# A transformer layer on one core: joining two products of one weight part into one 512-column matmul, and making two weight sums by accumulating DMA

## The chip, the cores and the metric

The kernel runs on one core of a Trainium2 chip. The metric is the device time of one execution in microseconds (us). Of the kernel before there are three runs, and beside them one profiled execution with its trace.

## The reference

One layer of a decoder on 512 tokens with 2048 features, in float32. What matters here is that nearly all of it is products of weights with activations:

```python
h    = rmsnorm(x, attn_norm_g)
proj = h @ w_in                      # 2048 -> 9216: u, v_sgu, q, k, v_att, g_a, g_b
y_a  = chunked_spatial_gating(gelu(u), rmsnorm(gelu(v_sgu)), w_s, b_s)
y_b  = stick_breaking_attention(rmsnorm(q), rmsnorm(k), v_att)
x    = x + (sigmoid(g_a) * (y_a @ w_up_a) + sigmoid(g_b) * (y_b @ w_up_b)) @ w_o
h    = rmsnorm(x, ffn_norm_g)
x    = x + (silu(h @ w_gate_half) * (h @ w_up_half)) @ w_ffn_out     # 2048 -> 2 * 5632 -> 2048
ple  = p @ w_ple
x    = x + sigmoid(rmsnorm(x, ple_norm_g) @ w_ple_gate) * ple
```

## The kernel before

Activations lie with features in partitions and tokens along the row. Every float32 operand is split into two float32r parts, high and low (`hi`, `lo`; `whi`, `wlo` for weights), and every product is three matmuls that add up in PSUM (`mm3`, L244 to L247): high weights by high activations, high weights by low activations, low weights by high activations. The first two have the same stationary operand.

A *unit* is two row tiles (256 rows) of the contraction, an output *pair* is two tiles of 128 features by 512 tokens. A plain unit (kind P) is four block products of 512 columns, so 12 matmuls. A Strassen unit (kind S) is seven half-size products of 256 columns in Winograd's form, so 21 matmuls. For it the weights become seven blocks of 128 columns: three as they are loaded, four that are sums. There are 766 Strassen units: 264 in the combined projection, 32 in the output projection, 344 in the first feed-forward product, 91 in the three passes of the second, 35 in the last gate. The other products are plain.

Weights come two units at a time (a *double*). `Weights` (L273) issues one DMA of 512 KB (L255) on the sync engine's queue (SP) into one of three raw blocks, and then, in steps that are interleaved with those of the next double: ScalarE (ACT) copies the three loaded blocks to `whi` (L312, 128x768), VectorE (DVE) makes two sums (L292, 128x512), subtracts for `wlo` (128x768), makes the third sum (128x256) and the fourth (L321, 128x256), ACT copies the four sums to `whi` (L323, 128x1024), and DVE makes their `wlo` (128x1024). A slot is a raw block with its `whi` and `wlo`; there are three, and the next DMA into a raw block waits until DVE has read it. `next_weights` (L345) prepares up to two doubles ahead.

`Pair.add` (L525) issues the matmuls. A Strassen pair keeps products P1 and P6 in PSUM bank `psp`, P7 and P4 in `psq`, P2 and P3 in `psy`, P5 in half of `psr`; `psy`, `psp`, `psq` exist twice, `psr` and `small` once, which makes eight banks. When the Strassen units of a pair are all issued, `mix` (L549) joins the products to the outputs: two copies by ACT (L553, L554) and four operations of DVE (L555 to L560), then `rest` adds the bank `psy` (L584).

Work beside the products (attention, gating, norms, forms of the activations) is issued by `tick`, once a unit, and kept behind that unit on each engine. A scheduler orders the instructions of each engine by their place in the program and by priorities; `Weights.to` raises the priority of the weights' steps.

Of the kernel before, what the change touches and what calls it, by code (L numbers as in the profile page):

```python
# [12 lines left out]
F32 = mybir.dt.float32  # L13
# [17 lines left out]
# Units by Strassen's products (S) and by plain ones (P) where they are mixed.  # L31
# [5 lines left out]
WHOLES = 13056  # L37
# [12 lines left out]
#   C11 = P1 + P2   C12 = P1 - P6 + P5 + P3   C21 = P1 - P6 + P7 - P4   C22 = P1 - P6 + P7 + P5  # L50
# A unit of the weights lies in DRAM as [A21 | A22 | A11 | A12].
# [3 lines left out]
def hybrid_layer(  # L55
# [5 lines left out]
    w_in: bass.AP,  # L61
    wsT: bass.AP,
# [16 lines left out]
    psm = ctx.enter_context(tc.tile_pool(name="psm", bufs=2, space=PSUM))  # L79
# [6 lines left out]
    # ---- SBUF that the phases share out among themselves: operands of float32r products in one  # L86
    # ---- tile, everything else in another
# [11 lines left out]
    class Arena:  # L99
# [4 lines left out]
        def take(self, n, how="low"):  # L104
            """Up from the bottom, at the lowest of the equal places, or down from the top."""
# [32 lines left out]
    def fits(sizes):  # L138
        """Whether these blocks can be had, with some room left over."""
# [17 lines left out]
    banks = iter(range(1 << 30))  # L157
    count = iter(range(1 << 30))
    psr = psa.tile([P, T], F32, name="psr")
    r_banks = [psr]  # L160

    def bank():
        tag = ("psy", "psp", "psq")[next(banks) % 3]
        return psm.tile([P, T], F32, tag=tag, name=nm(tag))
# [17 lines left out]
    def tick():  # L182
        """One unit more is issued. What is due now stays behind it on every engine."""
# [16 lines left out]
    class Staged:  # L200
        """The steps of a generator, one a unit, or all at once when the result is asked for."""
# [47 lines left out]
    slots = deque()  # L249

    def weight_tiles(src):
        """A slot, to be put back once its products are issued, with the weights as they are."""
        slot = slots.popleft()
        raw = slot[0].f(0, src.shape[1])
        nc.sync.dma_start(out=raw, in_=src)  # L255
        return slot, raw, slot[1], slot[2]
# [16 lines left out]
    class Weights:  # L273
# [10 lines left out]
        def steps(self):  # L284
# [9 lines left out]
            def nothing():  # L294
                pass
# [990 lines left out]
```

## Time and profile before

| | |
|---|---|
| Runs | 2731.14, 2731.86, 2733.67 us; median 2731.86 |
| Profiled execution, its span from the first to the last instruction | 2735.7 us |
| TensorE (PE) busy / weight loads (PEld) | 2714.8 / 2566.8 us, 19616 each |
| VectorE (DVE), ScalarE (ACT), GpSimd (POOL) busy | 2173.4, 1273.9, 68.4 us |
| DMA moved | 378.56 MB, read from DRAM 328.23 MB |

Three rates say what to look for in the trace: how far apart matmuls start (their busy times overlap, so the busy share of PE says little), how far apart DVE's instructions start, and how long a DMA takes from its issue until it has landed. The stages follow one another: the combined projection with attention under it up to about 790 us, the merging of the branches and the output projection to about 1230 us, the first feed-forward product to about 2090 us, the three passes of the second to about 2590 us, then the gate.

### The profile page before, as it was taken

Reading aid. Unit: us, or ns where it says so; the run is one execution under the profiler, and the core shown is the slowest. Engines: PE = TensorE matmul, PEld = TensorE weight load, DVE = VectorE, ACT = ScalarE, POOL = GpSimd, SP = SyncE. Lnnn points to the kernel's source line nnn. Section 1 sums busy time; section 2 is a strip of 40 time slices with the busy share of each in tenths; the row PEclk is TensorE's granted clock in tenths of the full one; section 3 lists DMA queues with packets and bytes.
Section 4 is the critical chain, followed back from the end, with each engine's and each line's share of the span. In section 5 each row is a group of like instructions: output and inputs, shape, how many; then the busy total and the mean of one; then the engine's idle time right before and its main releaser. Section 6 shows DMA issues by size and latency. Waiting matters only on the chain.

```text
span 2735.7 us, 48535 instructions
## 1 busy us (share of the span) xinstructions
PE 2714.8 (99%) x19616; PEld 2566.8 (94%) x19616; DVE 2173.4 (79%) x3457; ACT 1273.9 (47%) x1950; POOL 68.4 (2%) x130
## 2 busy tenths in 40 slices
PE   9999999999999999999999999999999999999999
PEld 7899999999998889989999999999999998988898
DVE  7677778787887667698888888888889677788887
ACT  7645555554544333374443444444345344343533
POOL 0100001010100000000000000000000000000000
PEclk9999999999999999999999999999999999999999
DMA  5333333333335444454333333333334445465654
GB/s 197 103 122 101 111 99 108 108 109 116 108 111 186 144 145 155 144 196 142 114 121 116 119 119 117 118 118 119 118 119 158 158 140 174 161 216 193 219 170 143
DMA packets 114416, 378.56 MB, mean 138 GB/s; under 512 B 12816, under 2 KB 15120, under 8 KB 114192
## 3 DMA queue, kind: packets, MB, share of 16 engines
q1 hardware_dynamic: 114192, 375.47, 42.8%
q8 instruction: 153, 2.51, 0.4%
q14 instruction: 71, 0.58, 0.1%
HBM read 328.23 MB, written 47.19 MB: 137 GB/s over the span
## 4 chain that ended last, share of the span: by engine, by line
issue 50%; PE 46%; DVE 1%; DMA 1%; ACT 1%; POOL 0%; POOLq 0%; DVEq 0%; ACTq 0%; SPq 0%
PE psy L245 5%; PE psy L246 5%; PE psy L247 5%; PE psq L247 4%; PE psp L247 4%; PE psq L246 4%; PE psp L246 4%; PE psp L245 4%; PE psq L245 4%; PE psr L247 1%; PE psr L245 1%; PE psr L246 1%; PE small L246 1%; PE small L247 1%; PE small L245 1%
## 5 line engine op out<-in xcount | busy, mean ns | idle before, releaser
L292 DVE TENSOR_TENSOR wlo<-wholes,whi 128x1024 fp32r<-128x1024 f32 (+3 forms) x943 | 991.2, 1054 | 365.7 <-ACT whi L312 291.0
L312 ACT ACTIVATE whi<-wholes 128x768 fp32r<-128x768 f32 (+1 forms) x397 | 327.1, 824 | 687.5 <-issue 333.6
L245 PE MATMUL psy<-parts,whi 128*128 128x256 f32 (+1 forms) x1956 | 600.4, 307 | 7.1 <-ACT whi L301 6.1
L246 PE MATMUL psy<-parts,whi 128*128 128x256 f32 (+1 forms) x1956 | 600.2, 307 | 0.0
L247 PE MATMUL psy<-parts,wlo 128*128 128x256 f32 (+1 forms) x1956 | 599.2, 306 | 0.0
L245 PE MATMUL psp<-parts,whi 128*128 128x256 f32 (+1 forms) x1706 | 516.4, 303 | 0.5 <-ACT whi L323 0.5
L247 PE MATMUL psp<-parts,wlo 128*128 128x256 f32 (+1 forms) x1706 | 502.0, 294 | 1.8 <-DVE wlo L292 1.8
L247 PE MATMUL psq<-parts,wlo 128*128 128x256 f32 (+1 forms) x1702 | 500.3, 294 | 2.0 <-DVE wlo L292 2.0
L246 PE MATMUL psp<-parts,whi 128*128 128x256 f32 (+1 forms) x1706 | 501.0, 294 | 0.0
L246 PE MATMUL psq<-parts,whi 128*128 128x256 f32 (+1 forms) x1702 | 500.7, 294 | 0.2 <-DVE parts L242 0.2
L245 PE MATMUL psq<-parts,whi 128*128 128x256 f32 (+1 forms) x1702 | 500.5, 294 | 0.0
L292 DVE TENSOR_TENSOR wholes<-wholes 128x256 f32<-128x256 f32 (+2 forms) x794 | 427.2, 538 | 5.5 <-DMA wholes<-w_gate 2.5
L323 ACT ACTIVATE whi<-wholes 128x1024 fp32r<-128x1024 f32 (+1 forms) x397 | 403.7, 1017 | 14.0 <-DVE wholes L321 14.0
L245 PEld LDWEIGHTS psy<-parts,whi 128*128 128x128 f32 x1956 | 374.3, 191 | 22.8 <-ACT whi L301 6.1
L247 PEld LDWEIGHTS psy<-parts,wlo 128*128 128x128 f32 x1956 | 374.2, 191 | 16.9
L246 PEld LDWEIGHTS psy<-parts,whi 128*128 128x128 f32 x1956 | 374.3, 191 | 15.9 <-DVE parts L242 0.7
L245 PEld LDWEIGHTS psp<-parts,whi 128*128 128x128 f32 x1706 | 326.5, 191 | 12.8 <-issue 1.7
L246 PEld LDWEIGHTS psp<-parts,whi 128*128 128x128 f32 x1706 | 326.3, 191 | 12.3 <-issue 1.7
L247 PEld LDWEIGHTS psp<-parts,wlo 128*128 128x128 f32 x1706 | 325.9, 191 | 9.6 <-DVE wlo L292 2.4
L247 PEld LDWEIGHTS psq<-parts,wlo 128*128 128x128 f32 x1702 | 326.0, 192 | 9.3 <-DVE wlo L292 2.8
L246 PEld LDWEIGHTS psq<-parts,whi 128*128 128x128 f32 x1702 | 325.9, 192 | 8.0 <-DVE parts L242 1.2
L245 PEld LDWEIGHTS psq<-parts,whi 128*128 128x128 f32 x1702 | 325.9, 191 | 7.2 <-issue 0.2
(139 smaller groups left out, 3369.8 us busy)
## 6 DMA issues: line engine op xcount, KB each, us to landing
wholes<-w_ffn_in SPq DMA_DIRECT2D x176, 512.0 KB, 3.9
wholes<-w_in SPq DMA_DIRECT2D x132, 512.0 KB, 3.9
wholes<-w_ffn_out SPq DMA_DIRECT2D x73, 512.0 KB, 3.7
wholes<-w_o SPq DMA_DIRECT2D x32, 512.0 KB, 4.1
wholes<-x SPq DMA_DIRECT2D x32, 512.0 KB, 5.3
wholes<-w_gate SPq DMA_DIRECT2D x25, 512.0 KB, 5.0
hid<-out SPq DMA_DIRECT2D x44, 256.0 KB, 2.0
wholes<-hid SPq DMA_DIRECT2D x22, 512.0 KB, 4.3
```

Source lines behind the costliest of these rows:

```text
L245: nc.tensor.matmul(ps, sh, mh, start=start, stop=False)
L246: nc.tensor.matmul(ps, sh, ml, start=False, stop=False)
L247: return nc.tensor.matmul(ps, sl, mh, start=False, stop=stop)
L292: return nc.vector.tensor_tensor(out=out, in0=a, in1=b, op=ALU.subtract)
L312: in_turn(nc.scalar.activation(h[:, :, 0:3], raw[:, :, 1:4], AF.Copy))
L323: nc.scalar.activation(h[:, :, 3:7], s, AF.Copy))
```

## The change

**Products.** In five of the seven Strassen products (P1, P6, P7, P5, P4) the matmuls of the high weights with the high and with the low activations become one of 512 columns, whose moving operand is a two-piece pattern over both parts (`both`). Each such product has a PSUM bank of its own: the left half takes high by high and low by high, the right half high by low. P2 and P3 stay as three matmuls each in halves of a sixth bank. A unit has 5 x 2 + 2 x 3 = 16 matmuls in place of 21, and streams as many columns. A double's two units now alternate product by product. All products draw on one pool of seven banks, and `small` is the eighth.

**Mixing.** The two halves of a bank have to be added, so `mix` becomes four copies by ACT and ten operations of DVE (eight of 256 columns, two of 512). It is a generator whose steps are issued between the products of the pair's last double.

**Weight sums.** Signs are turned so that all sums are additions. Two of the four sums (A21 + A22, A21 + A11) are made by DMA: block A21 is loaded twice into the places of the sums, the other three blocks by a second DMA, and then a DMA on POOL's queue with `accum_op=add` adds A22 and A11 onto them, read from DRAM again. DVE makes the other two. Then ACT copies five blocks at once (128x1280) and two later (128x512), and DVE splits them in the same shapes. The blocks lie by kind of block rather than by unit, in SBUF and in DRAM, for which the weights are laid out anew on the host; the first three outputs have an array of their own (`w_first`).

**Pipeline.** The raw block (`landings`, three of 3584 columns) and the split operands (`slots`, three) are handed out apart. Loads run several doubles ahead, as far as there are landings; `prepare_early` and `prepare_late` set the steps before and within a double's products.

```diff
-P1, P2, P3, P4, P5, P6, P7 = (1, 0), (2, 2), (6, 3), (0, 6), (3, 4), (5, 5), (4, 1)
+PRODUCTS = (2, 0), (0, 5), (5, 1), (4, 4), (1, 6), (3, 2), (6, 3)
+LOADED = {"S": slice(1, 6), "P": slice(0, 4)}
+SUMMED = slice(0, 7, 6)
...
     class Weights:
...
-            self.slot, self.raw, self.hi, self.lo = weight_tiles(src)
...
+            self.land = landings.popleft()
+            raw = self.blocks(self.land.f())
+            if kind == "P":
+                nc.sync.dma_start(out=raw, in_=src)
+            else:
+                nc.sync.dma_start(out=raw[:, 4:6],
+                                  in_=src[:, 0:1].to_broadcast([P, 2, n * P]))
+                nc.sync.dma_start(out=raw[:, 1:4], in_=src[:, 1:4])
...
+            def landed():
+                if self.kind == "S":
+                    nc.gpsimd.dma_start(out=raw[:, 4:6], in_=self.src[:, 1:3], accum_op=ALU.add)
...
             def high():
-                in_turn(nc.scalar.activation(h[:, :, 0:3], raw[:, :, 1:4], AF.Copy))
...
+                self.slot = slots.popleft()
+                self.hi, self.lo = (self.blocks(t) for t in self.slot)
+                split(LOADED[self.kind], True)
...
+            def sums():
+                if self.kind == "S":
+                    for o, i, j in ((0, 4, 2), (6, 0, 3)):
+                        in_turn(nc.vector.tensor_tensor(out=raw[:, o], in0=raw[:, i],
+                                                        in1=raw[:, j], op=ALU.add))
...
+            def rest():
+                split(LOADED[self.kind], False)
+                if self.kind == "S":
+                    split(SUMMED, True)
+                    split(SUMMED, False)
+                landings.append(self.land)
...
     def next_weights():
-        ws = prepared.popleft()
-        ahead(2)
...
+        ahead(1)
+        return prepared.popleft().get()
+
+    def prepare_early():
+
+        if prepared:
+            prepared[0].to(4)
+        if len(prepared) > 1 and (slots or prepared[1].step > 1):
+            prepared[1].to(3)
+
+    def prepare_late():
+
+        if len(prepared) > 1 and prepared[1].step > 1:
+            prepared[1].to(4)
+        ahead(8)
+        if len(prepared) > 3:
+            prepared[3].to(1)
...
+    def both(h, l):
+
+        a, b = sorted((h, l), key=lambda x: x.offset)
+        return bass.AP(a.tensor, a.offset,
+                       [list(a.ap[0]), [b.offset - a.offset, 2], list(a.ap[1])])
...
-            for ps, s, e, (w, x) in (
-                (self.p[:, :256], start, False, P1), (self.p[:, 256:], False, stop, P6),
-                (self.q[:, :256], start, False, P7), (self.q[:, 256:], False, stop, P4),
-                (self.y[:, :256], start, False, P2), (self.y[:, 256:], False, y_stop, P3),
-                (self.r, start, stop, P5),
-            ):
-                ws, ms = slice(w * P, (w + 1) * P), slice(x * 256, (x + 1) * 256)
-                mark(mm3(ps, wh[:, ws], wl[:, ws], xh[:, ms], xl[:, ms], s, e))
+            prepare_early()
...
+            for i, (w, x) in enumerate(PRODUCTS):
+                ps = self.banks[min(i, 5)]
+                for u, ((wh, wl), (xh, xl)) in enumerate(zip(ws, xs)):
+                    h, l = (t[:, x * 256 : (x + 1) * 256] for t in (xh, xl))
+                    s, e = start and u == 0 and i < 6, stop and u == n - 1 and i != 5
+                    if i < 5:
+                        nc.tensor.matmul(ps, wh[:, w], both(h, l), start=s, stop=False)
+                        mark(nc.tensor.matmul(ps[:, :256], wl[:, w], h, start=False, stop=e))
+                    else:
+                        half = ps[:, (i - 5) * 256 : (i - 4) * 256]
+                        mark(mm3(half, wh[:, w], wl[:, w], h, l, s, e))
+                if stop:
+                    next(mix)
+                if i == 2:
+                    prepare_late()
+                if i in TICKS[n]:
+                    tick()
```

How the instructions move is shown at three places of the first feed-forward product. The first is TensorE (PE) at a product within a Strassen unit. Before (the end of P1, then P6, then the start of P7; the number behind a tile's name tells its buffers apart):

```order
L247 MATMUL psp_12829<-parts,wlo_80 128x256
L245 MATMUL psp_12829<-parts,whi_79 128x256 [waits Activation_49]
L246 MATMUL psp_12829<-parts,whi_79 128x256
L247 MATMUL psp_12829<-parts,wlo_80 128x256 [waits DVE_49]
L245 MATMUL psq_12830<-parts,whi_79 128x256
```

Now (P1 of both units of a double, then the start of P6):

```order
L557 MATMUL ps_11617<-parts,whi_78 128x512 [waits Activation_49]
L558 MATMUL ps_11617<-parts,wlo_79 128x256 [waits DVE_49]
L557 MATMUL ps_11617<-parts,whi_78 128x512
L558 MATMUL ps_11617<-parts,wlo_79 128x256
L557 MATMUL ps_11618<-parts,whi_78 128x512 [waits DVE_49]
L558 MATMUL ps_11618<-parts,wlo_79 128x256
```

L245 and L246 have become one matmul of twice the columns, L247 has stayed as L558, and the first matmul into a bank waits for DVE, which empties that bank of the pair before.

The second is VectorE (DVE) where a pair ends. Before (`out` is the output being mixed, `psp`, `psq`, `psy` its banks, `wholes` holds raw weights and their sums):

```order
L555 TENSOR_TENSOR out_12385<-out_12385,psp_12181 128x256 [waits DMAHW6_49,Activation_49]
L557 TENSOR_TENSOR out_12385<-out_12385,psq_12182 128x256 [waits DVE_49,PE_49]
L292 TENSOR_TENSOR wlo_78<-wholes,whi_77 128x2x384 [waits PE_49,Activation_49]
L292 TENSOR_TENSOR wholes<-wholes 128x2x128
L292 TENSOR_TENSOR wlo_80<-wholes,whi_79 128x2x512 [waits Activation_49]
L558 TENSOR_TENSOR out_12385<-out_12385,p_876_12386 128x2x256 [waits DVE_49,Activation_49]
L321 TENSOR_TENSOR wholes<-wholes 128x2x128 [waits DVE_49]
L560 TENSOR_TENSOR out_12385<-out_12385,psq_12182 128x256 [waits DVE_49]
L584 TENSOR_TENSOR out_12385<-out_12385,psy_12180 128x512 [waits PE_49]
```

Now:

```order
L582 TENSOR_TENSOR out_10991<-out_10991,ps_10853 128x256 [waits DMAHW5_49,DMAHW1_49,Activation_49]
L582 TENSOR_TENSOR out_10991<-out_10991,ps_10854 128x256 [waits Activation_49]
L582 TENSOR_TENSOR out_10991<-out_10991 128x256 [waits DVE_49]
L582 TENSOR_TENSOR out_10991<-out_10991,ps_10855 128x256 [waits Activation_49]
L303 TENSOR_TENSOR wlo_77<-wholes,whi_76 128x1280
L303 TENSOR_TENSOR wlo_77<-wholes,whi_76 128x2x256 [waits Activation_49]
L582 TENSOR_TENSOR out_10991<-out_10991 128x256 [waits DVE_49]
L582 TENSOR_TENSOR p_1061_10996<-p_1061_10996,ps_10856 128x256 [waits Activation_49]
L582 TENSOR_TENSOR out_10991<-out_10991,ps_10857 128x256 [waits DVE_49,PE_49]
L582 TENSOR_TENSOR out_10991<-out_10991,p_1061_10996 128x2x256 [waits DVE_49]
L582 TENSOR_TENSOR out_10991<-out_10991,ps_10857 128x256
L582 TENSOR_TENSOR out_10991<-ps_10858,out_10991 128x512 [waits DVE_49,PE_49]
```

The mixing has grown from five instructions to ten, and one double's split stands in its middle, so the banks of P5 and P4 come free behind it.

The third is the transfers of weights. Before, on SP's queue, one for each double:

```order
L255 DMA wholes<-w_ffn_in 128x1024 [waits DMAHW2_49,DMAHW6_49,DVE_49,Activation_49]
L255 DMA wholes<-w_ffn_in 128x1024 [waits DMAHW4_49,DVE_49,Activation_49]
L1143 DMA hid_11553<-out_15409 128x512 [waits DVE_49]
L255 DMA wholes<-w_ffn_in 128x1024 [waits DMAHW5_49,DVE_49,Activation_49]
L255 DMA wholes<-w_ffn_in 128x1024 [waits DMAHW6_49,DVE_49,Activation_49]
```

Now on SP's queue, two for each double:

```order
L1184 DMA hid_10654<-out_10991 128x512 [waits DMAHW4_49,DVE_49]
L283 DMA wholes<-w_ffn_in 128x2x256 [waits DMASW3_49,DVE_49]
L285 DMA wholes<-w_ffn_in 128x768 [waits DMAHW7_49,DMAHW6_49]
L417 DMA wholes<-hid_10654 128x1024 [waits DMAHW4_49]
L283 DMA wholes<-w_ffn_in 128x2x256 [waits DMAHW0_49,DMASW4_49,DVE_49]
L285 DMA wholes<-w_ffn_in 128x768 [waits DMAHW1_49]
```

and on POOL's queue, which has no instruction in this stage before, one for each double:

```order
L296 DMA wholes<-w_ffn_in 128x512 [waits DMAHW1_49,DMASW6_49,DVE_49]
L296 DMA wholes<-w_ffn_in 128x512 [waits DMAHW3_49,DMASW7_49,DVE_49]
L296 DMA wholes<-w_ffn_in 128x512 [waits DMASW0_49,DMAHW5_49,DVE_49,Activation_49]
L296 DMA wholes<-w_ffn_in 128x512 [waits DMAHW7_49,DMASW1_49,DVE_49]
L296 DMA wholes<-w_ffn_in 128x512 [waits DMAHW2_49,DMASW2_49,DVE_49]
```

One transfer per double has become three on two queues, and the third waits for the landing of the first (DMAHW); in the program it is issued one double behind it.

More of the change, by code (lines that the diff above doesn't have):

```diff
@@ L155, in small_bank @@
         return psa.tile([P, T], F32, tag="small", name=nm("small"))
[L157 to L160, printed above, removed]
     def bank():
-        tag = ("psy", "psp", "psq")[next(banks) % 3]
-        return psm.tile([P, T], F32, tag=tag, name=nm(tag))
+        return psm.tile([P, T], F32, tag="ps", name=nm("ps"))
     clock = [0]
@@ L632, in hybrid_layer @@
     for i in range(3):
-        slots.append((take(1024, "high"), wp.tile([P, 2 * 7 * P], F32R, name=f"whi{i}"),
-                      wp.tile([P, 2 * 7 * P], F32R, name=f"wlo{i}")))
+        landings.append(take(2 * 7 * P, "high"))
+        slots.append(tuple(wp.tile([P, 2 * 7 * P], F32R, name=f"{n}{i}")
+                           for n in ("whi", "wlo")))
     ple_spill = {}
@@ L1168, in hybrid_layer @@
             x1 = load(spill["x1", j]) if c == len(PASSES) - 1 else None
-            pr = pair(units, last=j == KU - 1, plain=j == 0)
+            pr = pair(units, last=j == KU - 1, plain=j == 0, at=first)
             if before is None:
```

319 lines of the change are left out of this document (157 added, 162 removed).

## The prediction

> **What bounds the kernel now.** I read the page first, then who waited for whom on TensorE (PE), then the starts of its matmuls in the timeline.
>
> ```profile
> span 2735.7 us, 48535 instructions
> PE 2714.8 (99%) x19616; PEld 2566.8 (94%) x19616; DVE 2173.4 (79%) x3457; ACT 1273.9 (47%) x1950; POOL 68.4 (2%) x130
> PEclk9999999999999999999999999999999999999999
> q1 hardware_dynamic: 114192, 375.47, 42.8%
> ...
> PE psy L245 <- ACT whi L301: 6.1, 1, 6.1
> PE small L710 <- DVE diag L708: 2.7, 3, 1.8
> PE psq L247 <- DVE wlo L292: 2.0, 2, 1.5
> ```
>
> PE is busy throughout at full granted clock, and the longest waits for another engine add up to 6.1 + 2.7 + 2.0 = 10.8 us. So PE's own pace sets the time: what counts is how far apart matmuls start, not how long one is shown.
>
> ```profile
> 1499.82 0.28 PE L245 MATMUL psr<-parts,whi 128*128 128x256 f32 x1
> ...
> 1502.34 0.28 PE L245 MATMUL psr<-parts,whi 128*128 128x256 f32 x1
> ...
> 900.05 0.39 PE L245 MATMUL psq<-parts,whi 128*128 128x512 f32 x1
> ...
> 901.41 0.39 PE L245 MATMUL psp<-parts,whi 128*128 128x512 f32 x1
> ...
> 2126.94 0.28 PE L247 MATMUL psr<-parts,wlo 128*128 128x256 f32 x1
> 2127.06 0.40 PE L245 MATMUL psy<-parts,whi 128*128 128x512 f32 x1
> ```
>
> The first two rows are the same matmul of successive Strassen units, 21 starts apart: 2.52 us, 0.120 each. The next two are six starts of 512 columns apart: 1.36 us, 0.227 each. Twice the columns cost 0.107 more, not 0.120, so some 0.013 of each start does not depend on the columns. In the last two rows a 256-column matmul ahead of a 512-column one keeps its 0.12: mixing widths costs nothing.
>
> **What the joined products save.** Per unit five pairs of 2 x 0.120 become one of 0.227: 5 x 0.013 = 0.065 us, so a unit takes 5 x (0.227 + 0.120) + 6 x 0.120 = 2.455 in place of 2.520. P1 and P6 each have one L245 matmul of a unit in bank p, so the next row counts 1532 / 2 = 766 units:
>
> ```profile
> L245 PE MATMUL psp<-parts,whi 128*128 128x256 f32 x1532 | 448.6, 293 | 0.5 <-ACT whi L323 0.5
> ```
>
> 766 x 0.065 = **49.8 us** off. The trace shows no moving operand of two pieces; its bounds are 0.227 (all rows of 512 columns) and 0.240 (as before, nothing saved). I take 0.227, the nearest in width.
>
> The Trainium skill (TensorE: Matmul & The Clock Gate, Back-to-back issue gap) gives N/2.4 + 2.5 ns for a warm matmul, so an estimate of 109 and 216 ns. By it a join would save 2.5 ns and the change 766 x 5 x 2.5 ns = 9.6 us. The rows show 120 and 227, a fixed part five times as large, and the measurement decides.
>
> **VectorE (DVE): about even.** Its starts, one after the other without idle time:
>
> ```profile
> 1509.72 0.69 DVE L292 TENSOR_TENSOR wholes<-wholes 128x512 f32<-128x512 f32 x1
> 1510.33 0.69 DVE L1139 TENSOR_TENSOR out<-out,wholes 128x512 f32<-128x512 f32 x1
> 1510.93 0.95 DVE L292 TENSOR_TENSOR wlo<-wholes,whi 128x768 fp32r<-128x768 f32 x1
> 1511.80 0.42 DVE L292 TENSOR_TENSOR wholes<-wholes 128x256 f32<-128x256 f32 x1
> 1512.13 0.69 DVE L1142 TENSOR_TENSOR out<-out 128x512 f32<-128x512 f32 x1
> 1512.73 1.22 DVE L292 TENSOR_TENSOR wlo<-wholes,whi 128x1024 fp32r<-128x1024 f32 x1
> 1513.87 0.42 DVE L321 TENSOR_TENSOR wholes<-wholes 128x256 f32<-128x256 f32 x1
> ```
>
> From start to start: 512 columns 0.60, 768 0.87, 256 0.33, 1024 1.14; 1280 by the same slope 1.41. A double costs 0.60 + 0.87 + 0.33 + 1.14 + 0.33 = 3.27 now, and 2 x 0.33 + 1.41 + 0.60 = 2.67 after. Mixing a pair costs 3 x 0.33 + 2 x 0.60 = 2.2 now, and 8 x 0.33 + 2 x 0.60 = 3.8 after. A pair of four doubles gives 2.4 us back and pays 1.6. Where few units are Strassen's it turns round. By stages:
>
> ```profile
> 1500.00:1800.00 300.00, 300.00 (x2502) 300.00 (x2502) 253.21 (x403) 124.99 (x165) 0.00 (x0) 1.00 0.38 119
> 2440.00:2590.00 150.00, 149.46 (x865) 131.91 (x864) 134.23 (x212) 73.89 (x101) 1.92 (x1) 1.00 0.58 199
> ```
>
> (Columns: stretch, length, busy us of PE, PEld, DVE, ACT, POOL, clock, DMA share, GB/s.) In the first feed-forward product DVE is 84% busy (253.21 of 300), and its work falls with PE's. In the third pass a pair has three Strassen units (one double, one single) and four plain: 3 x 2.52 + 48 x 0.227 = 18.5 us, DVE 89% of it, 16.5. It gains about 0.7 (1.6 less 0.6 for the double and some 0.3 for the single) and PE gets 0.2 shorter: 17.2 of 18.3, 94%. I charge the seven pairs there 0.7 each, **+5 us**; nothing and twice that are the ends.
>
> **ScalarE (ACT).**
>
> ```profile
> L323 ACT ACTIVATE whi<-wholes 128x1024 fp32r<-128x1024 f32 x369 | 386.4, 1047 | 11.7 <-DVE wholes L321 11.7
> L312 ACT ACTIVATE whi<-wholes 128x768 fp32r<-128x768 f32 x369 | 312.4, 847 | 640.7 <-PE psy L246 318.5 <-issue 300.0 <-DMA wholes<-w_gate 8.1
> L554 ACT ACTIVATE out<-psp 128x256 f32<-128x256 f32 x102 | 39.1, 383 | 204.6 <-PE psp L247 199.2 <-DMA wholes<-w_ffn_out 2.7 <-DMA outT<-out 2.7
> ```
>
> 256 columns more cost 0.20, so 1280 take 1.25 and 512 some 0.65, the sum as now. Two more copies of 0.38 for each of 112 Strassen pairs (33 + 8 + 43 + 21 + 7) are 85 us on an engine that is 47% busy: nothing, with its idle time as the cover.
>
> **The banks.** PE now waits for DVE's mixing before it reuses a bank. The last double of a pair takes 0.694 a product (2 x 0.347), 4.91 in all. P4 is done at 3.47, and the next pair takes that bank for its sixth product, at 4.91 + 5 x 0.694 = 8.4. DVE starts at about 1.3 (P1 at 0.69, its latency, a copy of 0.38) and does before that bank is free 8 x 0.33 + 0.60 of mixing and 1.41 + 0.60 of a split, 5.25: free at 6.6. The cover is 1.8 us; I charge nothing. If DVE is late by 2.3 us at every pair, 0.5 x 112 = 56 us are lost.
>
> **The weights' supply** is what can turn the sign.
>
> ```profile
> wholes<-w_ffn_in SPq DMA_DIRECT2D x176, 512.0 KB, 3.9
> wholes<-x SPq DMA_DIRECT2D x32, 512.0 KB, 5.3
> hid<-out SPq DMA_DIRECT2D x44, 256.0 KB, 2.0
> ...
> L811 POOL TENSOR_TENSOR rr<-ms,expo 128x4 f32<-128x4 f32 x16 | 17.6, 1098 | 191.9 <-DVE ms L809 191.9
> ```
>
> Three landings serve one double each, and a double lasts 4.91, so a landing must come round in 14.7 us. On its way: load 3.9; POOL's issue, not in the trace, 1.1 as POOL's longest frequent instruction; the accumulate, not in the trace either, between 2.0 (a transfer of its 256 KB) and 7.8 (its 256 KB read, the destination read and rewritten: two 512 KB transfers); ACT 1.25; DVE 2.67. I take 3.9 for the accumulate, the 512 KB row, since it handles two operands of 256 KB. Sum 3.9 + 1.1 + 3.9 + 1.25 + 2.67 = 12.8: it fits by 1.9 us, and to 5.8 us for the accumulate nothing is lost. What queues behind a waiting accumulate is the next one and, in the projection, POOL's small attention steps, which ACT waits for; I charge 1 us there. Loads may run late by what stands ahead on SP, yet a double is split a whole double before PE wants it.
>
> The Trainium skill (DMA: Bandwidth & Descriptors, Anatomy of one DMA) fits a DMA from POOL's queue as 2.0 us plus bytes over 436 GB/s, an estimate of 2.6 us for 256 KB; no run here shows it yet, and by it the landing would fit by 3.2 us.
>
> By bytes: a double moved 512 KB and now counts 256 + 384 + 2 x 256 = 1152 KB, 655,000 bytes more in 4.91 us, 133 GB/s. The stretch from 1500 us has a share of 0.38 at 119 GB/s; after, (119 + 3 + 133) x 0.38 / 119 = 0.81. The third pass: 3 x 0.33 MB more in 18.3 us, 54 GB/s, 0.74. Below 1, but transfers will land later.
>
> **Sum.** -49.8 + 5 + 1 = -44 us on the profiled 2735.7, so 2692. The runs' median 2731.86 lies 3.8 under that span: **2688 us**. Own range 2671 (the 10.8 us of waits go too, and the third pass costs nothing) to 2710 (waits of 0.2 us at each of 112 pairs).
>
> **Rivals.**
>
> *The supply becomes the bound (slower).* One mechanism: load and accumulate outlast the landing's turn. It starts at 5.8 us for the accumulate. The doubles are 369 by the rows of L323, and 766 - 2 x 369 = 28 single units count half: 383. The 44 us are spent when a double is late by 0.115, a turn by 0.35, so from 6.2 us on. At 7.8 a turn takes 16.7, 2.0 too long, 0.66 a double, +253: 2688 + 253 = 2941. At 6.5 it is 0.7 / 3 x 383 = +89: 2777. For it: the margin is 1.9 us in 14.7, and the DMA share doubles. Against it: landings are handed out several doubles ahead, and 256 KB can land in 2.0. Chance 0.19.
>
> *Late mixing.* PE waits for a bank at every pair: by 0.5 us, 2688 + 56 = 2744; by 0.25, 2716. For it: DVE works in order, and a split stands in the middle of the mixing. Against it: 1.8 us of cover. Chance 0.08, of which 0.05 ends faster, 0.02 within 0.2%, 0.01 slower.
>
> *The join saves little or nothing.* A moving operand of two pieces starts every 0.240, as two matmuls did: 2731.9 + 6 = 2738; with 0.2375, 2728. Against it: the fixed 0.013 stands at every start of both widths. Chance 0.05, counted as no change. (The second figure is what the fixed part of 2.5 ns in the skill's formula would leave.)
>
> **Chances.** A measurement of this kernel can tell 0.2%, 5.5 us, from no change. The forecast has 0.68; so faster 0.68 + 0.05 = 0.73, the same 0.02 + 0.05 = 0.07, slower 0.19 + 0.01 = 0.20. The range 2666 to 2740 leaves out most of the supply's rival, and little below.
>
> **What would show it.** Right: pairs of 512 and 256 columns start 0.347 apart; about 15,790 matmuls; accumulates land in under 5.8 us; PE's waits stay near 10 us; DVE 90% or more in the third pass. Wrong: PE waits for `whi` of L301 or `wlo` of L303 in every double, with ACT waiting for POOL's DMA; or PE waits for DVE at L557 where a pair begins; or joined matmuls at 0.240.

## The result and the profile after

The changed kernel takes **2866.32 us** (median of four runs, 2862.72 to 2886.46), the kernel before 2732.73 (median of four): a ratio of 1.0503 (95% interval 1.0470 to 1.0536), 134 us slower. The prediction said 2688. Its profiled execution spans 2866.5 us, 130.8 more than that of before. One run of ffn_back, further down, took 2901.26 us at a granted clock of 0.851 in place of 0.998 and is left out of that kernel's figures. The page of the changed kernel, in the lines that were shown of before, with the queues and the chain:

```profile
span 2866.5 us, 43349 instructions
PE 2740.1 (96%) x15786; PEld 2371.2 (83%) x15786; DVE 2169.2 (76%) x3663; ACT 1346.5 (47%) x2181; POOL 440.1 (15%) x527
PEclk9999999999999999999999999999999999999999
q1 hardware_dynamic: 241872, 425.70, 46.7%
q0 software_dynamic: 60752, 100.43, 21.5%
...
PE 47%; DVE 25%; DMA 18%; issue 5%; ACT 4%; POOL 1%; SPq 0%; ACTq 0%; DVEq 0%; POOLq 0%
```

The same chain in the kernel before:

```profile
issue 50%; PE 46%; DVE 1%; DMA 1%; ACT 1%; POOL 0%; POOLq 0%; DVEq 0%; ACTq 0%; SPq 0%
```

The mean granted clock is 0.993 after 0.999 and PE still shows 96%, but the chain that ended last, nearly all "issue" and PE before, now runs through DVE for a quarter and through DMA for 18%. A share of 96% says little here, since busy times overlap. The same stretch of the first feed-forward product says more (columns as in the prediction):

```profile
1500.00:1800.00 300.00, 283.90 (x1766) 250.69 (x1765) 224.15 (x385) 123.42 (x179) 47.84 (x55) 0.99 0.74 185
2550.00:2720.00 170.00, 156.08 (x749) 128.28 (x748) 143.82 (x237) 72.78 (x110) 15.77 (x15) 0.96 0.66 204
```

A double now has 32 matmuls, so 1766 in 300 us are one double in 300 / (1766 / 32) = 5.44 us. Before it was 2502 of 42 each, 5.04; the prediction wanted 4.91. PE no longer sets the pace. Who waits for whom in the changed kernel (total, times, longest; us):

```profile
PE ps L557 <- DVE p L582: 28.5, 34, 1.4
PE ps L248 <- DVE out L582: 20.6, 40, 0.7
PE ps L557 <- ACT whi L301: 16.5, 13, 2.9
...
DVE wholes L314 <- DMA wholes<-w_ffn_in: 183.7, 44, 6.7
DVE out L582 <- ACT out L579: 173.5, 99, 5.9
...
ACT whi L301 <- DMA wholes<-w_ffn_in: 172.5, 53, 7.8
```

ACT and DVE stand 172.5 and 183.7 us at the accumulating transfer, and PE shows waits for mixing (L582) and for split weights (L301), 65.6 us in these three rows where some 10 were forecast for all. The first two rows look like the rival of late mixing, but L314 and L582 share one queue: while L314 stands at the transfer, the mixing behind it is late as well. The transfers of this kernel, issue to landing:

```profile
wholes<-w_ffn_in SPq DMA_DIRECT2D x172, 384.0 KB, 5.2
...
wholes<-w_ffn_in SPq DMA_DIRECT2D x172, 256.0 KB, 4.4
wholes<-w_ffn_in POOLq DMA_DIRECT2D x172, 256.0 KB, 4.6
```

One turn of a landing, from the timelines of the changed kernel's queues (start, length, engine, line; in square brackets the idle time before it and what ended it):

```profile
1501.62 0.38 SPq L283 DMA_DIRECT2D wholes<-w_ffn_in  x1
...
1508.12 0.86 POOL L296 DMA_DIRECT2D wholes<-w_ffn_in  x1 [5.31 <-DMA wholes<-w_ffn_in]
...
1512.96 1.28 ACT L301 ACTIVATE whi<-wholes 128x1280 fp32r<-128x1280 f32 x1 [0.18 <-DMA wholes<-w_ffn_in]
...
1509.76 0.88 DVE L314 TENSOR_TENSOR wholes<-wholes 128x256 f32<-128x256 f32 x2 [4.77 <-DMA wholes<-w_ffn_in]
1511.48 0.75 DVE L582 TENSOR_TENSOR out<-out,ps 128x256 f32<-128x256 f32 x2 [0.83 <-ACT out L579]
...
1517.60 0.42 DVE L314 TENSOR_TENSOR wholes<-wholes 128x256 f32<-128x256 f32 x1
...
1518.87 2.09 DVE L303 TENSOR_TENSOR wlo<-wholes,whi 128x1280 fp32r<-128x1280 f32 x2
...
1520.38 0.38 SPq L283 DMA_DIRECT2D wholes<-w_ffn_in  x1
```

Loaded at 1501.62, accumulated onto from 1508.12 (POOL stood 5.31 us at a load), copied at 1512.96, summed only from 1517.60, free at 1520.38: 18.8 us. DVE first stood 4.77 us at the transfer of the landing before, and then had that landing's mixing and splits to make up. Over the whole stage (the k-th load, accumulate, copy and split taken together, without the first few loads, which run far ahead) the turn has a mean of **16.4 us**: 5.0 from load to accumulate (4.4 until the load has landed, 0.7 of waiting), 6.6 from there to ACT's copy (5.05 for issue and transfer, 1.55 of waiting), 4.8 until the next load. Three landings give a double every 5.47 us, and 172 doubles 940 us of the 949.0 that the stage lasts.

Where the time lies, by stages of the program (us, each up to its last store; the sums lie some 8 us over the spans, for every kernel alike). Each row is one profiled execution, and some of these lie off the median of their kernel: before's span is 3.8 us above it, free_sums's run 2.8 below, land4's 14 below, ffn_grouped's 8 above, after_grouped's 8 below, split_back's 6 below. Differences of a few us between rows say little. Beside before and after stand the experiments of the next section:

| kernel | projection | merge, output, first pair | first FFN product | three passes | gate |
|---|---|---|---|---|---|
| before | 856.6 | 383.4 | 875.9 | 463.5 | 164.7 |
| after | 874.7 | 390.6 | 949.0 | 494.1 | 165.5 |
| free_sums | 847.5 | 387.0 | 867.6 | 471.2 | 165.0 |
| pool_plain | 856.2 | 389.2 | 874.5 | 486.7 | 165.4 |
| dve_sums | 866.2 | 386.8 | 915.8 | 484.9 | 174.1 |
| split_back | 887.8 | 390.8 | 956.8 | 494.3 | 165.7 |
| land4 | 875.4 | 390.7 | 869.2 | 487.6 | 184.7 |
| five4 | 884.1 | 389.2 | 898.9 | 490.8 | 162.7 |
| grouped_free | 842.5 | 386.1 | 857.8 | 472.2 | 163.8 |
| ffn_grouped | 863.1 | 385.5 | 858.0 | 466.8 | 191.8 |
| ffn_back | 860.2 | 384.4 | 858.3 | 469.1 | 172.4 |
| after_grouped | 874.6 | 389.3 | 962.0 | 495.4 | 164.5 |

Of the 130 us, 73 are lost in the first feed-forward product, 31 in the passes of the second, 18 in the projection. (A landing is 2 x 7 x 128 = 1792 columns; where the text on the change says 3584, that is wrong.)

### The profile page after: what moved, and what is told of

Same layout as the page of the kernel before. It is cut to its first block, busy times and chain, and to the rows that moved or that the text cites. A ratio compares the mean times of both kernels' runs of the same rounds, so it can differ in the third digit from the quotient of the medians.

```text
span 2866.5 us, 43349 instructions
## 1 busy us (share of the span) xinstructions
PE 2740.1 (96%) x15786; PEld 2371.2 (83%) x15786; DVE 2169.2 (76%) x3663; ACT 1346.5 (47%) x2181; POOL 440.1 (15%) x527
## 3 DMA queue, kind: packets, MB, share of 16 engines
q0 software_dynamic: 60752, 100.43, 21.5%
## 4 chain that ended last, share of the span: by engine, by line
PE 47%; DVE 25%; DMA 18%; issue 5%; ACT 4%; POOL 1%; SPq 0%; ACTq 0%; DVEq 0%; POOLq 0%
PE ps L557 14%; DVE wlo L303 10%; PE ps L248 8%; PE ps L249 8%; PE ps L250 8%; DMA wholes<-w_ffn_in 8%; PE ps L558 7%; DVE out L582 7%; DMA wholes<-w_in 3%; DVE wholes L314 2%; ACT whi L301 2%; DMA wholes<-sum 2%; DMA x<-wholes 1%; DMA sum<-wholes 1%; DVE parts L245 1%
## 5 line engine op out<-in xcount | busy, mean ns | idle before, releaser
L557 PE MATMUL ps<-parts,whi 128*128 128x512 f32 x3830 | 1395.1, 404 | 51.4 <-DVE p L582 28.5
L301 ACT ACTIVATE whi<-wholes 128x512 fp32r<-128x512 f32 (+4 forms) x950 | 857.0, 918 | 1025.7 <-DVE wholes L314 322.8
L558 PE MATMUL ps<-parts,wlo 128*128 128x256 f32 x3830 | 1073.2, 283 | 4.5 <-DVE wlo L303 4.3
L303 DVE TENSOR_TENSOR wlo<-wholes,whi 128x512 fp32r<-128x512 f32 (+4 forms) x950 | 962.0, 1047 | 93.0 <-ACT whi L301 92.0
L557 PEld LDWEIGHTS ps<-parts,whi 128*128 128x128 f32 x3830 | 722.7, 189 | 227.7 <-DVE p L582 42.2
L248 PE MATMUL ps<-parts,whi 128*128 128x256 f32 (+1 forms) x2538 | 831.8, 329 | 42.9 <-DVE out L582 20.6
L249 PE MATMUL ps<-parts,whi 128*128 128x256 f32 (+1 forms) x2538 | 831.4, 328 | 6.5 <-DVE parts L245 6.5
L250 PE MATMUL ps<-parts,wlo 128*128 128x256 f32 (+1 forms) x2538 | 827.4, 327 | 3.0 <-DVE wlo L303 3.0
L558 PEld LDWEIGHTS ps<-parts,wlo 128*128 128x128 f32 x3830 | 726.0, 190 | 17.3 <-DVE wlo L303 9.3
L248 PEld LDWEIGHTS ps<-parts,whi 128*128 128x128 f32 x2538 | 482.4, 190 | 113.4 <-issue 35.0
L249 PEld LDWEIGHTS ps<-parts,whi 128*128 128x128 f32 x2538 | 483.9, 191 | 48.0 <-DVE parts L245 10.1
L250 PEld LDWEIGHTS ps<-parts,wlo 128*128 128x128 f32 x2538 | 483.6, 191 | 43.4 <-DVE wlo L303 4.1
L314 DVE TENSOR_TENSOR wholes<-wholes 128x256 f32<-128x256 f32 (+1 forms) x794 | 326.9, 412 | 240.1 <-DMA wholes<-w_ffn_in 183.7
L582 DVE TENSOR_TENSOR out<-out,ps 128x256 f32<-128x256 f32 x510 | 206.5, 416 | 174.3 <-ACT out L579 173.5
L245 DVE TENSOR_TENSOR parts<-wholes,parts 128x1024 fp32r<-128x1024 f32 (+3 forms) x129 | 122.6, 964 | 24.0 <-ACT parts L244 23.7
L1181 ACT ACTIVATE out<-out 128x512 f32<-128x512 f32 x44 | 27.9, 633 | 183.8 <-DVE out L1180 183.7
L582 DVE TENSOR_TENSOR out<-out 128x256 f32<-128x256 f32 x204 | 86.3, 423 | 3.2
```

The costliest lines, as they stand in the source:

```text
L245: nc.vector.tensor_tensor(out=lo, in0=src, in1=hi.bitcast(F32), op=ALU.subtract))
L248: nc.tensor.matmul(ps, sh, mh, start=start, stop=False)
L249: nc.tensor.matmul(ps, sh, ml, start=False, stop=False)
L250: return nc.tensor.matmul(ps, sl, mh, start=False, stop=stop)
L301: in_turn(nc.scalar.activation(h, r, AF.Copy))
L303: in_turn(nc.vector.tensor_tensor(out=self.lo[:, blocks], in0=r, in1=h.bitcast(F32), op=ALU.subtract))
```

## The experiments

All changes are against the changed kernel unless another is named; ratios are to the kernel before, with the 95% interval.

**free_sums: the supply made free.** Both summed blocks come by one ordinary load, and block A21 is left out of them.

```diff
-                nc.sync.dma_start(out=raw[:, 4:6],
-                                  in_=src[:, 0:1].to_broadcast([P, 2, n * P]))
+                nc.sync.dma_start(out=raw[:, 4:6], in_=src[:, 1:3])
...
-                if self.kind == "S":
-                    nc.gpsimd.dma_start(out=raw[:, 4:6], in_=self.src[:, 1:3], accum_op=ALU.add)
+                pass
```

> Left out: block A21 in the two sums, which are plain copies of A22 and A11 loaded by SP; no accumulate, no second chain link, same instructions on PE, ACT and DVE. Supply theory (load, accumulate and split outlast a landing's turn): the turn falls from 16.4 to some 10 us, PE sets the pace at 0.354 us a joined product, so 2736 - 23 and a few waits: 2705 to 2740 us. Rival, late mixing (DVE's ten operations a pair hold PE's banks whatever the supply): nothing of that changes, 2830 us or more.

2734.55 us, 1.0005 (0.9995 to 1.0014). The way of making the sums costs 2866.3 - 2734.6 = 132 us. Late mixing as a cause of its own falls: banks, mixing and join are the same here, and the waits for mixing (L580 in this kernel) are gone from PE's list, which begins:

```profile
PE ps L248 <- ACT whi L299: 7.6, 2, 6.2
PE ps L248 <- ACT parts L244: 4.9, 4, 1.8
PE ps L555 <- ACT whi L299: 4.7, 4, 1.8
```

But even with nothing to pay, the joined products bring no gain as a whole. In the first feed-forward product:

```profile
1500.00:1800.00 300.00, 300.00 (x1934) 271.90 (x1933) 247.42 (x422) 140.26 (x198) 0.00 (x0) 1.00 0.48 145
```

1934 matmuls are one double in 4.96 us: 0.07 less than before, where 0.13 was forecast.

**dve_sums: the joined products alone.** One load of four blocks, all four sums by DVE.

```diff
...
-                nc.sync.dma_start(out=raw[:, 1:4], in_=src[:, 1:4])
+                nc.sync.dma_start(out=raw[:, 0:4], in_=src)
...
+                if self.kind == "S":
+                    in_turn(nc.vector.tensor_tensor(
+                        out=raw[:, 4:6], in0=raw[:, 0:1].to_broadcast([P, 2, n * P]),
+                        in1=raw[:, 1:3], op=ALU.add))
```

> The joined products alone: the two sums by DVE (128x512, 0.60 us a double), one load of 512 KB, no DMA on POOL's queue. Supply theory: a landing's turn is 4 us of load and some 5 to 6 of sums and splits, PE sets the pace, DVE 91% busy in the first feed-forward product: 2715 to 2760 us. Late-mixing theory: DVE has 2.4 us more a pair, so banks come free later still: 2870 us or more.

2821.73 us, 1.0318 (1.0302 to 1.0333), between its two expectations. In the same stretch DVE is busy 273.27 us of 300, the 91% that was expected, but the time is 62 us over the upper end that went with it:

```profile
1500.00:1800.00 300.00, 289.09 (x1818) 255.03 (x1817) 273.27 (x457) 127.48 (x188) 0.00 (x0) 1.00 0.37 115
```

Over the whole kernel PE's longest wait is now for ACT's copies of the weights,

```profile
PE ps L558 <- ACT whi L298: 35.4, 59, 1.9
```

and these copies in turn wait 637.7 us in all for the sums that DVE makes (L305). So it looks as if the longer mixing had room only where DVE gives sums away; that DVE's work is the limit here is read from these waits, and no run took it out by itself.

**split_back: the sums by DMA alone.** The join is taken back within the bank.

```diff
-                        nc.tensor.matmul(ps, wh[:, w], both(h, l), start=s, stop=False)
+                        nc.tensor.matmul(ps[:, :256], wh[:, w], h, start=s, stop=False)
+                        nc.tensor.matmul(ps[:, 256:], wh[:, w], l, start=False, stop=False)
```

> The weight sums by DMA alone: each joined matmul is two of 256 columns into the two halves of its bank, 21 matmuls a unit as before, 0.360 us a product. Supply theory: PE has slack, so the time stays within 10 us of 2866. Theory that the two-piece operand costs PE its time: it returns to below 2760. If PE's pace still decided: 766 x 5 x 0.006 = 23 us more, 2889.

2895.59 us, 1.0596 (1.0564 to 1.0628): the loss is all there without the join, and 29 us more, beyond the 10 that the supply theory allowed and near the 2889 of PE's pace; after_grouped, below, speaks against that reading, since a shorter PE gains nothing there. Its landing's turn is 16.56 us (16.41 in the changed kernel), which accounts for the feed-forward product, where 7.8 us were added, but the projection lost 13 and I can't say by what.

**pool_plain: the accumulate's place kept, its adding taken out.** The same transfer on POOL's queue, without `accum_op`; A21 is missing from two sums.

```diff
-                    nc.gpsimd.dma_start(out=raw[:, 4:6], in_=self.src[:, 1:3], accum_op=ALU.add)
+                    nc.gpsimd.dma_start(out=raw[:, 4:6], in_=self.src[:, 1:3])
```

> The change with a plain DMA in place of the accumulating one (same queue, same wait for the load, same bytes), so the two sums lack A21. Theory that the accumulate's own length is what is too long: packets of 0.178 us become 0.085, the turn falls under 14.9 and the time to 2735 to 2770. Theory that the chain of two transfers is too long whatever the second one does: 2800 or more.

2764.59 us, 1.0115 (1.0100 to 1.0130). Of the 132 us, 2866.3 - 2764.6 = 102 are due to the adding itself; the other 30 go with the second transfer, its stop at POOL and its bytes, which free_sums leaves out together. The queue and the landing in this kernel:

```profile
q0 software_dynamic: 30864, 100.43, 11.4%
...
wholes<-w_ffn_in POOLq DMA_DIRECT2D x172, 256.0 KB, 3.3
```

For the same 100.43 MB the accumulating form has 60752 packets in place of 30864 and 21.5% of the DMA engines' time in place of 11.4%; it lands 1.3 us later. The turn is 15.08 us, shorter by 1.33, but not by the landing alone: 0.5 less lies ahead of the accumulate (the loads land sooner too, in 3.3 us for 4.4), 0.6 between it and ACT's copy, 0.2 behind. And 15.08 is close to the 14.9 that three doubles take at PE's own pace of 4.97 (land4). The Trainium skill (DMA: Bandwidth & Descriptors, Anatomy of one DMA) gave an estimate of 2.6 us for such a transfer: the plain one takes 3.3 here, the accumulating one 4.6.

**land4: a fourth landing, during the first feed-forward product only.**

```diff
+    landings.append(take(2 * 7 * P, "high"))
     for m in range(KH):
+        if m == KH - 2:
+            spare.append("back")
...
-                landings.append(self.land)
+                if spare and spare[0] == "back":
+                    spare.clear()
+                    give(self.land)
+                else:
+                    landings.append(self.land)
```

> A fourth landing during the first feed-forward product only (given back before the three passes). Supply theory with the latency of the chain as the limit: a turn may last 19.9 us against 16.4 needed, so that stage falls from 949 to about 870 to 885 us and the whole to 2785 to 2805. Rival: the DMA engines' throughput is the limit (0.74 share): the stage stays above 930, the whole 2850 to 2870.

2815.64 us, 1.0286 (1.0261 to 1.0312). The stage falls from 949.0 to 869.2 us, as with free sums, while accumulates land no sooner (5.0 us); the whole is above the expectation. In the profiled execution, which at 2801.77 us is 14 us faster than the median, the gate took 184.7 us in place of 165.5 (see ffn_back); what the other runs lost besides isn't known.

```profile
1500.00:1800.00 300.00, 300.00 (x1931) 271.71 (x1930) 247.49 (x423) 138.78 (x195) 52.20 (x60) 1.00 0.79 200
```

The DMA engines are busy 0.79 here, against 0.74 in the changed kernel. Their throughput was not the limit, then: it was how many landings there are for a turn of that length.

**five4: smaller landings, four of them everywhere.** Sums in place, five blocks for each.

```diff
-                    for o, i, j in ((0, 4, 2), (6, 0, 3)):
+                    for o, i, j in ((1, 3, 1), (2, 1, 2)):
...
+    for i in range(4):
+        landings.append(take(2 * 5 * P, "high"))
```

> All of the change, but the two DVE sums overwrite A11 and A12 in the landing after their split, so that a landing has five blocks, and four landings fit where three did, in all stages. Supply theory: a turn may last 19.9 us, as in land4 but everywhere: the first feed-forward product near 870, the projection and the passes gain what they lost, 2730 to 2760. Rival, the engines' throughput or the later split decides outside that stage: near land4's 2816.

2816.36 us, 1.0297 (1.0280 to 1.0315), the figure of the rival, though the first feed-forward product lost too (898.9 us, land4 869.2). With the sums in place, DVE has to split the five blocks before it may sum, and ACT and DVE wait for each other far longer than in the changed kernel (there 322.8 us for the sums and 92.0 for the copies):

```profile
ACT whi L302 <- DVE wholes L316: 672.2, 309, 8.3
...
DVE wlo L304 <- ACT whi L302: 410.3, 508, 4.7
```

**one_piece_free: is it the two-piece operand?** free_sums, with the joined matmul reading 512 neighbouring columns, which are not the right ones.

```diff
-                        nc.tensor.matmul(ps, wh[:, w], both(h, l), start=s, stop=False)
+                        nc.tensor.matmul(ps, wh[:, w], xh[:, x * 256 : x * 256 + 512] if x < 6 else xh[:, 1280:1792], start=s, stop=False)
```

> free_sums (2734.6 us), and the joined matmul reads 512 neighbouring columns of the high part instead of 256 of the high and 256 of the low: right shape, other values. Theory that the second piece costs the time: the spacing of a joined product goes from 0.354 (0.236 + 0.118) to 0.347 and the time to about 2710. Theory that the alternation of widths costs it: spacing and time stay, 2730 to 2738.

2734.15 us, 1.0001 (0.9992 to 1.0010), as free_sums: the operand's two pieces cost nothing. Its joined matmul still holds PE for 0.236 and the 256-column one behind it for 0.118 (medians of the starts), as in the changed kernel:

```profile
1502.03 0.39 PE L557 MATMUL ps<-parts,whi 128*128 128x512 f32 x1
1502.26 0.28 PE L558 MATMUL ps<-parts,wlo 128*128 128x256 f32 x1
1502.37 0.40 PE L557 MATMUL ps<-parts,whi 128*128 128x512 f32 x1
1502.61 0.28 PE L558 MATMUL ps<-parts,wlo 128*128 128x256 f32 x1
1502.72 0.40 PE L557 MATMUL ps<-parts,whi 128*128 128x512 f32 x1
```

**grouped_free: does the alternation of widths cost?** free_sums, with both units' joined matmuls first, then both narrow ones.

```diff
+                for u, ((wh, wl), (xh, xl)) in enumerate(zip(ws, xs) if i < 5 else ()):
+                    h, l = (t[:, x * 256 : (x + 1) * 256] for t in (xh, xl))
+                    nc.tensor.matmul(ps, wh[:, w], both(h, l), start=start and u == 0, stop=False)
...
-                        nc.tensor.matmul(ps, wh[:, w], both(h, l), start=s, stop=False)
```

> As free_sums (A21 is left out of the two sums, so the weights' supply is free), with one more change: in each of the five joined products of a double, the 512-column matmuls of both units are issued first and the 256-column ones after them, so the widths alternate half as often. If a 512-column matmul that stands beside a 256-column one costs about 6 ns more (0.236 and 0.118 against 0.227 and 0.120), half of these 6 ns return: some 12 us of 2734.5, so 2715 to 2728. If the cost lies in the joined matmul itself, whatever stands beside it, the time stays at 2731 to 2738.

2715.97 us, 0.9934 (0.9920 to 0.9948): the same matmuls in another order save 18.6 us. Two joined products now take 0.70 in place of 0.71:

```profile
1502.49 0.63 PE L553 MATMUL ps<-parts,whi 128*128 128x512 f32 x2
1502.96 0.40 PE L558 MATMUL ps<-parts,wlo 128*128 128x256 f32 x2
1503.19 0.63 PE L553 MATMUL ps<-parts,whi 128*128 128x512 f32 x2
```

and in the stretch from 1500 us:

```profile
1500.00:1800.00 300.00, 300.00 (x1956) 272.99 (x1955) 248.08 (x427) 142.18 (x201) 0.00 (x0) 1.00 0.48 148
```

1956 matmuls are a double in 4.91 us, the forecast's own figure. That the order is what counts is shown; why it does, is not.

**ffn_only, ffn_grouped, ffn_back: the change only where it can be paid for.** The first feed-forward product with joined products, accumulates and four landings; all else with DVE's sums and 256-column products in four banks. In short, for ffn_only (ffn_grouped adds the order above):

```diff
-            if kind == "P":
-                nc.sync.dma_start(out=raw, in_=src)
+            if not (kind == "S" and acc):
+                nc.sync.dma_start(out=raw[:, 0:4], in_=src)
...
-                self.banks = [bank() for _ in range(2 if kind == "P" else 6)]
+                self.banks = [bank() for _ in range(2 if kind == "P" else 6 if self.joined else 4)]
...
+                    if not self.joined:
+                        b, k = HALVES[i]
+                        mark(mm3(ps[:, k * 256 : (k + 1) * 256], wh[:, w], wl[:, w], h, l,
```

> The change only where its supply can be paid for: joined products, accumulating sums and a fourth landing in the first feed-forward product alone; in all other stages VectorE forms the sums and the products are two 256-column matmuls, as before the change, in four banks. If the landing's turn is all that is wrong in the first feed-forward product, that stage takes 865 to 872 us as with four landings (875.9 before the change) and the others what they took before the change or a little less: 2715 to 2735 in all. If the late supply also harms the stages that keep the older form (through the arrangement of the weights that both share), it stays above 2740.

> As ffn_only, with the matmuls of a joined product grouped by width over the two units of a double. If the alternation of widths costs 6 ns a joined matmul, 5 to 9 us less than ffn_only; if not, the same time within 4 us.

2762.39 us, 1.0102 (1.0088 to 1.0115), and 2751.24, 1.0066 (1.0052 to 1.0079). The order saves 11 us where 5 to 9 were expected, and the stage itself is as expected (868.4 and 858.0 for 875.9). ffn_only lies above 2740, as by the second alternative of its expectation; the projection and the merging cost some us too, but most of it is the gate, which takes 187.7 and 191.8 us. There PE stands while late operands are loaded, as in this piece of ffn_grouped's chain,

```profile
2595.77 6.11 DMA wholes<-x
```

and the granted clock is low where the gate begins:

```profile
2560.00:2580.00 20.00, 15.59 (x57) 11.26 (x56) 13.10 (x23) 9.12 (x14) 1.14 (x1) 0.72 0.52 172
```

Whichever landing came free first was given back, so the free room may have lain in pieces. ffn_back gives back the added one:

```diff
-                if spare and spare[0] == "back":
+                if spare[1:] and self.land is spare[0]:
```

> As ffn_grouped, but at the end of the first feed-forward product the fourth landing itself is given back, and not whichever landing comes free first, so that the other three stay where they were and the free room is in one piece. In ffn_grouped the gate at the end took 191.8 us in place of 164.7, with PE waiting while operands of x were loaded late. If that came of the free room lying in pieces, the gate takes 164 to 168 us again and the whole 2722 to 2732, below the kernel before; if it came of something else in the arrangement that all these kernels share, 2745 to 2755.

2738.06 us (median of eleven runs), 1.0015 (1.0006 to 1.0024), between its two expectations: the gate falls from 191.8 to 172.4, most of the way, but no further. The medians differ by 13 us, so a part of these 19 belongs to ffn_grouped's slower profiled execution. How the free room lay was argued from this, and no trace shows it. The first feed-forward product is 17.6 us shorter than in the kernel before, and the four other stages, in the older form, are together 17.9 us longer than in the kernel before, whose order of steps this one does not keep. No full version that beats the kernel before was found.

**after_grouped: the changed kernel in the grouped order.** The diff is that of grouped_free.

> The changed kernel with nothing else altered but the grouped order: in each joined product of a double the 512-column matmuls of both units first, then the 256-column ones. With the supply free this order saved 18.6 us of PE's pace (2734.55 to 2715.97). If the landing's turn alone sets the pace, PE only waits longer for the same weights: the first feed-forward product stays at 945 to 953 us and the whole at 2860 to 2872. If the turn itself hangs on PE's pace (VectorE mixes a pair only when its products are done, and the sums and splits of the weights stand behind that mixing), a part comes through, as the slower un-joined matmuls cost 29 us in split_back: 2846 to 2858.

2888.25 us, 1.0557 (1.0537 to 1.0578), outside both expectations: a shorter PE gains nothing while the supply sets the pace. The landing's turn is 16.63 us, and in the stretch from 1500 PE does 1748 matmuls:

```profile
1500.00:1800.00 300.00, 278.63 (x1748) 248.67 (x1747) 219.13 (x377) 122.04 (x179) 47.97 (x55) 0.99 0.74 182
```

Why it and split_back should be 20 to 30 us slower than the changed kernel stays open. In both the turn is longer between load and accumulate alone (5.3 us in place of 5.0), and the runs of the changed kernel themselves lie up to 24 us apart.

## Why the prediction was wrong

**The step that failed is the landing's turn: "Sum 3.9 + 1.1 + 3.9 + 1.25 + 2.67 = 12.8: it fits by 1.9 us".** The changed kernel shows 5.0 until the accumulate (3.9 in the sum), 6.6 from there to ACT's copy (1.1 + 3.9) and 4.8 for the splits (1.25 + 2.67): 1.1 + 1.6 + 0.9 = 3.6 us more, 16.4, and so 1.7 too long in place of 1.9 to spare. The term that was in doubt came out as forecast: issue and accumulate together take a mean of 5.05 us, 1.1 + 3.9 = 5.0 in the sum, and the median of 4.6 lies under the 5.8 at which, by the prediction, nothing would be lost. What the sum put at nothing is the waiting between steps, 0.7 us ahead of POOL and 1.55 ahead of ACT's copy; besides, the load takes 0.5 more and the splits 0.9. So the threshold was wrong, because the sum lets each step start at the moment when the one before it ends. In the trace each step stands in a queue in which order is kept: POOL at the next load, ACT at the transfer, DVE at L314 with the mixing and the next landing's splits behind it. What shows it: free_sums (132 us come back), pool_plain (102 of them by taking out the adding) and land4 (80 us in the one stage, by a landing more and the same slow transfers). No run took out one of the waits by itself, so how the 3.6 us are shared is read from the changed kernel's trace alone. The spread may have its part in them: of 165 accumulates of this stage 51 take over 5.8 us from issue to landing, the longest 8.2.

**The first rival happened in its outcome, not by its reason.** It priced a turn of 16.7 us at 2941, and the turn is 16.4; but the rival reached its turn by an accumulate of 7.8 us, and the accumulate took no longer than the sum had it. That the two turns nearly agree is luck. With 1.7 in place of 2.0 us too long, its rule gives 2688 + 1.7 / 3 x 383 = 2905. The 2866 are less since the projection lost 18 us and not the share of its 132 doubles, 75. The prediction gave it 0.19, on the ground that landings are handed out ahead. But handing out ahead adds no landing: a load still can't start before the landing of three doubles earlier has been split.

**The join was mis-sized: 0.065 us a unit, 49.8 in all.** "Mixing widths costs nothing" was read from one place, a narrow matmul ahead of a wide one, and the wide one's own length was not looked at there. In the order of the change a pair holds PE for 0.236 + 0.118 = 0.354, not 0.347: 0.006 saved where 0.013 was forecast, 23 us for 3830 of them. (The wide one's 0.236 is near the 0.2375 of the third rival, but that rival's reason was another.) In the first feed-forward product, where 344 units should have given 22 us, free_sums shows 8.3 and grouped_free 18.1. Direction and mechanism were right; the order of issue took nearly half of the size. The third rival's reason, the two-piece operand, is refuted by one_piece_free.

**What held.** DVE even: 2169.2 us busy after 2173.4. ACT: 73 us more, 85 forecast, hidden. The third pass: 159.8 in free_sums after 154.4, the +5 of the sum, though no run shows that DVE is the reason. DVE is busy 135.18 of 150 us there, 90%, and 143.82 of 170, 85%, in the changed kernel, where the supply stretches the pass; 94 was forecast. The DMA share of 0.81 at 4.91 us a double: 0.79 in land4 at 4.97. The banks: with free sums the mixing is on time. 15786 matmuls for 15,790.

**Not forecast.** With free sums the passes lose 7.7 us in all and the part from merging to the first pair 3.6, more than the 8.3 that the first product gains; the projection gains 9.1. Of the third pass's 5.4 the forecast knew, the rest I have not traced. The runs show no gain, 2734.55 after 2734.30. In the grouped order they gain 19 us (2715.97 after 2735.45), so even with free sums and without the loss by the order the 44 of the sum are not reached. The 1 us for POOL's attention can't be told from the rest: pool_plain's projection is 8.7 us longer than free_sums's, the plain transfers with it.

## What to carry to other kernels

A buffer's turn is not the sum of its steps' durations: take from the trace how long each step stands in its in-order queue, and where the margin is a tenth of the turn, call the sign open. Work that DMA takes from an engine can come back as latency and then needs one more buffer before it pays; here one landing more gave back all of the 73 us lost in its stage, though the whole stayed slower than before. And before a saving of a few nanoseconds an instruction is multiplied by thousands, look for a place in the trace where the instructions stand in the very order that the change gives them.

## What was not expected of the hardware

- A DMA that adds while it lands has twice the packets (60752 for 30864) and nearly twice the DMA time (21.5% for 11.4%) of the plain one with the same bytes, and lands in 4.6 us in place of 3.3 (medians). Its issue holds POOL for 0.87 us in place of 0.54.
- Matmuls of 512 columns that alternate with others of 256 take 0.354 us a pair (0.236 + 0.118), and 0.350 when two of each width stand together (0.70 for the four); 512 columns alone were 0.227 apart before, and 256 alone 0.120.
- In ffn_grouped the granted clock is 0.50 from 2568.8 to 2582.4 us, soon after 1.3 us in which PE was idle (from 2567.1), and matmuls of 512 columns start 0.43 us apart there, 0.23 once it is 1.00 again. That the idle time brings it on isn't shown: in the changed kernel PE is idle for 2.4 us at 106.9, and the clock stays at 1.00.
